# The decay matrix of a head pair: one exponential over 2048 columns in place of eight pieces

## The chip, the cores and the metric

The kernel runs on one core of a Trainium2 chip. The metric is the device time of one execution in microseconds, lower is better. Three executions of the kernel before took 2666.51, 2668.19 and 2668.41 us (median 2668.19).

## What is computed

One step of a hybrid encoder trunk (one layer here) over 384 token columns: one prompt of 256 tokens and eight running streams of 16 tokens. A combined projection gives a pooling branch, a state-space branch (SSD) and gates; both branches are projected, gated, added and projected again, and a squared-ReLU MLP follows. The part that matters here is the SSD scan, in which every head's products of C and B are weighted by a decay:

```
def step(h, inp):
    xc, dtc, Bc, Cc = inp
    cum = jnp.cumsum(dtc * A, axis=1)
    seg = cum[:, :, None] - cum[:, None, :]
    decay = jnp.exp(jnp.where(causal, seg, -jnp.inf))
    cb = jnp.einsum('btgn,bsgn->btsg', Cc, Bc)
    xdt = xc * dtc[..., None]
    y = jnp.einsum('btsgr,bsgrp->btgrp', cb[..., None] * decay, xdt)
    ...
```

There are 64 heads in 8 groups of 8; a head has 64 channels and a state of 128. A gated RMSNorm with SiLU(z) follows. All data are float32.

## The kernel before, in words

**Weights and matmuls.** Every weight block (128x1024 float32) is fetched by SyncE, then split in two parts: `wh` is a copy on ScalarE (ACT, L70) and `wl` the difference on VectorE (DVE, L71). TensorE (PE) multiplies wh by the high and low part of the activations and wl by the high part (L97 to L100 for projections with stationary weights, L149 to L151 for those with moving weights). There are three buffers each for the raw block, wh and wl. `take` keeps up to three split blocks ahead of the one in use, so the split of a block is called two blocks before its use.

**The SSD stage.** A loop over 8 head groups `g` runs, per group, ten projections (`x` for the conv: four blocks of channels, B and C; then four `z` projections) of two weight blocks each. Between the projections stand the small steps of the scan, each for a pair of column tiles (`Pair`, four heads; two pairs a group). The second pair of a group is finished at the head of the next group, the last one after the loop, around `gate_b`. PE's order is written out by hand: each lump of small matmuls and each half projection is put behind the one before (`chain`, `behind`, `lump`). The order on ACT and DVE comes from a planner, which takes the program's order as priority and fills in an instruction when its inputs are ready by the planner's own costs; so it is not the program's order. Each engine runs its list in order.

**The decay matrix E** (`eside`, L751 to L768). For a pair, E is 128x4x512: four heads, 512 columns each. Columns 0:128 are prompt half one with itself, 128:256 half one's influence on half two, 256:384 half two with itself, 384:512 the streams. `eside(S, q)` makes two of the four heads (q is 0 or 1). Its input `cbc` holds the running sum `cum` of the two heads, spread over the partitions by a DMA through DRAM that ACT's queue issues (`cload`). `tok` holds values per token and head; its rows 0 to 2 are cum of the three token blocks, row 9 is `nb`, made in `dt_phase` (L499), row 10 exp(cum) of the streams. Per head, columns 128:256 are Exp with the bias of row 9 (L756), and the other three blocks are Relu(tok - cbc), which keeps the differences from being negative (L758). Then Exp(-E) goes over columns 0:128 of the two heads (L766) and over columns 256:512 of the two (L767), and DVE multiplies the two heads by the masked products `cbm` (L768). E has one buffer, so the first write of a pair's E waits for the matmuls of the pair before (`t_Y`, L677), which read it.

**Where eside is called.** For the first pair of a group: `eside(S, 0)` after the last conv projection, `eside(S, 1)` after the projection z0, and `t_Y` after z3. For the second pair: `eside(.., 0)` after the next group's first conv projection, `eside(.., 1)` after its second, `t_Y` after its fifth. After the last group both are called one behind the other, ahead of `gate_b(0)`.

**Other instructions on the same queues.** ACT runs conv taps (L590), Silu of the conv (L596) and of z (L919), copies (L582 to L584) and the splits; when a function is not in the table set that is loaded, a table load (ACT_TABLE_LOAD) stands before it under the same line. DVE runs evacuations of PSUM (L576, L918), conv taps (L592), the scaling of the state by its decay (L771), its update (L794) and the splits.

**Transpositions through DRAM.** x and B are transposed in 32x32 blocks on DVE (L607), written to DRAM and read back by DMAs that GpSimd (POOL) issues (L612, L618).

Of the kernel before, what the change touches and what calls it, by code (L numbers as in the profile page):

```python
# [9 lines left out]
AF = mybir.ActivationFunctionType  # L10
ALU = mybir.AluOpType
# [3 lines left out]
P = 128  # L15
T = 384
TP = 256
# [16 lines left out]
def build(ctx, tc, io):  # L34
    nc = tc.nc
    v, s, te, gp, sy = nc.vector, nc.scalar, nc.tensor, nc.gpsimd, nc.sync
# [13 lines left out]
    def mmtile(name):  # L50
        return psm.tile([P, 512], F32, tag="mm", name=name)
# [4 lines left out]
    def behind(ins):  # L56
        return nullcontext() if ins is None else tc.issue_after(ins.ins)
# [24 lines left out]
    def woven(a):  # L82
        return a.rearrange("p (a n) -> p n a", a=2)

    def pairs(a):
        return a.rearrange("p (n a) -> p n a", a=2)

    def even_odd(a):
        return a.rearrange("p (n a) -> p a n", a=2)

    def halves(a):
        return a.rearrange("p (a n) -> p a n", a=2)
# [265 lines left out]
    tok = small.tile([P, 11, NH], F32, name="tok")  # L358
    decb = small.tile([P, NH, NB], F32, name="decb")
    with tc.tile_pool(name="phc", bufs=1, reuse_waits="tile") as pc, tc.tile_pool(name="phc2", bufs=2, reuse_waits="tile") as pc2:  # L360
# [3 lines left out]
        for i in range(2):  # L364
            b = pc.tile([P, 640], F32, name=f"pbuf{i}")[:, :519]
# [91 lines left out]
        def dt_phase(pb):  # L457
            ps = mmtile("pj_dt")[:, :T]
            for q in range(2):
                w = wpool.tile([P, 1024], F32, tag="w", name=f"w_dt{q}")  # L460
                hl = wpool.tile([P, 8, 2, NH], F32R, tag="wh", name=f"wh_dt{q}")
                wv = w[:, :512].rearrange("p (k n) -> p k n", k=8)
                sy.dma_start(w[:, :512], io["w_dt"][q])
                s.activation(hl[:, :, 0], wv, AF.Copy)
                v.tensor_tensor(hl[:, :, 1], wv, hl[:, :, 0].bitcast(F32), ALU.subtract)
                for k in range(8):
                    c = hl[:, k].rearrange("p a n -> p (a n)")
                    te.matmul(pairs(ps), c, woven(xg[q * 8 + k][0]), start=q + k == 0, stop=False)
                    te.matmul(pairs(ps), c, woven(xg[q * 8 + k][1]), start=False, stop=q * 8 + k == KD - 1)
            n64 = lambda nm: pb.tile([NH, T], F32, name=nm)  # L470
            dtb = vec[:NH, V_DTB : V_DTB + 1]
            alog = vec[:NH, V_ALOG : V_ALOG + 1]
            raw, ab, e, t1, t2, q = (n64(x) for x in ("raw", "ab", "e", "t1", "t2", "q"))
            nA = pb.tile([NH, 1], F32, name="nA")
            with behind(s.copy(halves(raw), even_odd(ps[NH:]))):
                s.activation(nA, alog, AF.Exp)
            v.tensor_tensor(halves(raw), even_odd(ps[:NH]), halves(raw), ALU.add)
            v.tensor_tensor(raw, raw, rstd[:NH], ALU.mult)
            s.activation(ab, raw, AF.Abs, bias=dtb)
            s.activation(e, ab, AF.Exp, scale=-1.0)  # L480
            v.tensor_scalar(t1, e, 2.0, None, ALU.add)
            v.reciprocal(t2, t1)
            v.tensor_tensor(t1, e, t2, ALU.mult)
            v.tensor_tensor(t2, t1, t1, ALU.mult)
            v.tensor_scalar(q, t2, 1.0 / 19.0, None, ALU.mult)
            for i in range(8, 0, -1):
                v.scalar_tensor_tensor(out=q, in0=q, scalar=1.0 / (2 * i + 1), in1=t2, op0=ALU.add, op1=ALU.mult)
            v.scalar_tensor_tensor(out=q, in0=q, scalar=1.0, in1=t1, op0=ALU.add, op1=ALU.mult)
            v.tensor_scalar(raw, raw, dtb, 0.0, ALU.add, ALU.max)
            dt, cum = n64("dt"), n64("cum")  # L490
            v.scalar_tensor_tensor(out=dt, in0=q, scalar=2.0, in1=raw, op0=ALU.mult, op1=ALU.add)
            dta, we, dtw = n64("dta"), n64("we"), n64("dtw")
            v.tensor_scalar(dta, dt, nA, -1.0, ALU.mult, ALU.mult)
            v.tensor_tensor_scan(cum, cst[:NH, C_SCAN : C_SCAN + T], dta, 0.0, ALU.mult, ALU.add)
            sy.dma_start(cum_scr, cum)
            nb = n64("nb")
            tot = pb.tile([NH, 1], F32, name="tot")
            v.tensor_tensor(tot, cum[:, 127:128], cum[:, 255:256], ALU.add)
            v.tensor_scalar(nb[:, :P], cum[:, :P], cum[:, 127:128], -1.0, ALU.subtract, ALU.mult)  # L499
            v.tensor_scalar(we[:, :P], cum[:, :P], tot, -1.0, ALU.subtract, ALU.mult)  # L500
            v.tensor_scalar(we[:, P:TP], cum[:, P:TP], cum[:, 255:256], -1.0, ALU.subtract, ALU.mult)
            cs = cum[:, TP:].rearrange("h (b t) -> h b t", b=NB)
            last = cs[:, :, TS_ - 1 : TS_]
            v.tensor_tensor(
                we[:, TP:].rearrange("h (b t) -> h b t", b=NB), last.to_broadcast([NH, NB, TS_]), cs, ALU.subtract
            )
            s.activation(we, we, AF.Exp)
            v.tensor_tensor(dtw, dt, we, ALU.mult)
            s.activation(nb[:, TP:], cum[:, TP:], AF.Exp)
            dec = pb.tile([NH, NB], F32, name="dec")  # L510
            s.activation(dec, last.squeeze(2), AF.Exp)
            sy.dma_start(dec_scr, dec)
            sy.dma_start(decb, dec_scr.partition_broadcast(P))
            srcs = [cum[:, i * P : i * P + P] for i in range(3)] + [dt[:, i * P : i * P + P] for i in range(3)]
            srcs += [dtw[:, i * P : i * P + P] for i in range(3)] + [nb[:, :P], nb[:, TP:]]
            return srcs
# [11 lines left out]
        for gi in range(4):  # L528
            for k4 in range(4):
                pool_tile(gi, k4)  # L530
                if gi and k4 == (gi == 1):
                    if gi == 1:
                        sg = gate_a(0)
                    pool_map(gi - 1, last[0])
        srcs = dt_phase(pc)
        pool_map(3)
        for nb in range(4):
# [18 lines left out]
    with tc.tile_pool(name="phd", bufs=2, reuse_waits="tile") as pd, tc.tile_pool(  # L556
# [5 lines left out]
        for i in range(3):  # L562
            b = pd1.tile([P, 24, 19], F32, name=f"cbuf{i}")
# [187 lines left out]
        def eside(S, q):  # L751
            if q == 0:
                S.E = pd.tile([P, 4, 512], F32, tag="E", name=f"E{S.nm}", bufs=1)
            for hh in (q * 2, q * 2 + 1):
                ch = S.cbcs[q][:, hh % 2]
                s.activation(S.E[:, hh, P:TP], ch[:, P:TP], AF.Exp, bias=tok[:, 9, S.h0 + hh : S.h0 + hh + 1])  # L756
                for b, e0 in enumerate((0, TP, T)):
                    s.activation(  # L758
                        S.E[:, hh, e0 : e0 + P],
                        ch[:, b * P : b * P + P],  # L760
                        AF.Relu,
                        bias=tok[:, b, S.h0 + hh : S.h0 + hh + 1],
                        scale=-1.0,
                    )
            Eq = S.E[:, q * 2 : q * 2 + 2]
            s.activation(Eq[:, :, :P], Eq[:, :, :P], AF.Exp, scale=-1.0)  # L766
            s.activation(Eq[:, :, TP:], Eq[:, :, TP:], AF.Exp, scale=-1.0)  # L767
            v.tensor_tensor(Eq, Eq, S.D.cbm.unsqueeze(1).to_broadcast([P, 2, 512]), ALU.mult)  # L768

        def dside(S):  # L770
            v.tensor_tensor(  # L771
# [79 lines left out]
        for g in range(G + 1):  # L851
            if g == G:
                xside(prev.p[1])
                eside(prev.p[1], 0)
                eside(prev.p[1], 1)
                dside(prev.p[1])
                gate_b(0, pd, "hs")
                py = mmtile("pp_last")
                lump(lambda: t_pp(prev.p[1], py))
                lump(lambda: t_yT(prev.p[1]))  # L860
                lump(lambda: t_Y(prev.p[1]))
                state(prev.p[1])
                final(prev.p[1])
                gate_b(1, pd, "hs")
                finish(prev)
                break
# [9 lines left out]
            if g:  # L876
                eside(prev.p[1], 0)
# [14 lines left out]
            S = D.p[0]  # L892
# [383 lines left out]
    with tc.tile_pool(name="phg", bufs=1, reuse_waits="tile") as pg, tc.tile_pool(  # L1276
# [9 lines left out]
        for c8 in range(NC):  # L1286
            hh = []
# [175 lines left out]
```

## Time and profile before

| what | value |
|---|---|
| median of three executions | 2668.19 us |
| the profiled execution, its own time | 2666.41 us |
| its span, first to last instruction | 2664.6 us |
| granted TensorE clock, mean | 0.999 |
| SSD stage and closing part, about | 420 to 1310 us of the span |
| one steady head group | 90 us, of which PE 89.3, DVE 77, ACT 61, POOL 25 |

How to read it: the busy row gives each engine's share of the span; the views of waits say which engine stood idle before which instruction, and until what; PEld are the weight loads of PE, which run beside its matmuls. A row of the timeline is the start, the duration, the engine, the line, the operation, what it writes and reads, and in brackets the idle time before it and what ended that.

### The profile page before, as it was taken

The page shows a single profiled execution, that of the slowest core. Times are in us where ns is not written, and L with a number is a line of the kernel's source. Part 1 is how long each engine was busy: PE and PEld are TensorE (multiplying, and loading weights), DVE is VectorE, ACT ScalarE, POOL GpSimd, SP SyncE. Part 2 cuts the span into 40 slices and gives each one's busy share as a digit, 9 for nine tenths or more (in the row PEclk, how much of TensorE's full clock was granted, in tenths as well). Part 3 has the DMA queues.
Part 4 walks back from the last instruction along what each step waited for, and adds up shares of the span by engine and source line. Part 5 has one row for each costly group of instructions (what it writes and reads, how often), then busy time and mean ns, then how long its engine had stood idle before and what let it go on. Part 6 is the DMA issues. An engine that isn't in the chain of part 4 may idle for free.

```text
span 2664.6 us, 38740 instructions
## 1 busy us (share of the span) xinstructions
PE 2639.9 (99%) x15405; PEld 2454.2 (92%) x15405; DVE 1528.4 (57%) x2148; ACT 1196.3 (45%) x1850; POOL 226.6 (9%) x350
## 2 busy tenths in 40 slices
PE   9999999999999999999999999999999999999998
PEld 9998888999999999978888888999999999999897
DVE  6585335788888988856334446534444444444446
ACT  6443225567676767645322235533233333323233
POOL 0000001223222322210000000000000000000000
PEclk9999999999999999999999999999999999999999
DMA  7444446556666666747544544444444444444443
GB/s 272 150 135 155 147 146 218 182 194 223 216 221 202 218 224 212 240 163 246 178 158 158 175 169 133 148 135 135 136 135 138 137 135 134 135 135 135 136 137 131
DMA packets 129141, 451.37 MB, mean 169 GB/s; under 512 B 17408, under 2 KB 24128, under 8 KB 123968
## 3 DMA queue, kind: packets, MB, share of 16 engines
q1 hardware_dynamic: 103552, 361.57, 41.2%
q0 software_dynamic: 18496, 72.64, 7.6%
q10 hardware_dynamic: 6912, 14.68, 1.7%
q8 instruction: 121, 1.98, 0.3%
q14 instruction: 60, 0.49, 0.1%
HBM read 404.49 MB, written 44.34 MB: 168 GB/s over the span
## 4 chain that ended last, share of the span: by engine, by line
PE 74%; issue 14%; DVE 7%; ACT 3%; DMA 1%; POOL 1%; DVEq 0%; ACTq 0%; POOLq 0%
PE pj_up L98 6%; PE pj_up L100 6%; PE pj_up L99 6%; PE wd L151 6%; PE wd L150 6%; PE wd L149 6%; PE pj_x L98 3%; PE pj_x L99 3%; PE pj_x L100 3%; PE pj_sp L150 3%; PE pj_sp L149 3%; PE pj_sp L151 3%; PE pj_z L100 2%; PE wo L151 2%; PE wo L149 2%
## 5 line engine op out<-in xcount | busy, mean ns | idle before, releaser
L98 PE MATMUL pj_up<-x1h,wh_up 128*128 128x384 f32 (+1 forms) x1024 | 333.7, 326 | 0.0
L99 PE MATMUL pj_up<-x1l,wh_up 128*128 128x384 f32 (+1 forms) x1024 | 333.4, 326 | 0.0
L100 PE MATMUL pj_up<-x1h,wl_up 128*128 128x384 f32 (+1 forms) x1024 | 333.4, 326 | 0.0
L71 DVE TENSOR_TENSOR wl_wd<-w_wd,wh_wd 128x1024 fp32r<-128x1024 f32 x126 | 154.4, 1225 | 240.4 <-ACT wh_wd L70 240.4
L149 PE MATMUL wd<-wh_wd,hh 128*128 128x512 f32 x756 | 286.5, 379 | 0.0
L150 PE MATMUL wd<-wl_wd,hh 128*128 128x512 f32 x756 | 286.5, 379 | 0.0
L151 PE MATMUL wd<-wh_wd,hl 128*128 128x512 f32 x756 | 286.5, 379 | 0.0
L70 ACT ACTIVATE wh_wd<-w_wd 128x1024 fp32r<-128x1024 f32 x126 | 133.1, 1057 | 322.2 <-PE wd L151 261.8
L70 ACT ACTIVATE wh_up<-w_up 128x1024 fp32r<-128x1024 f32 x126 | 133.1, 1057 | 292.2 <-PE pj_up L99 231.8
L71 DVE TENSOR_TENSOR wl_up<-w_up,wh_up 128x1024 fp32r<-128x1024 f32 x126 | 154.4, 1225 | 178.3 <-ACT wh_up L70 178.2
L98 PE MATMUL pj_x<-xgh,wh_x 128*128 128x384 f32 x768 | 252.0, 328 | 0.6 <-ACT wh_x L70 0.6
L100 PE MATMUL pj_x<-xgh,wl_x 128*128 128x384 f32 x768 | 250.6, 326 | 1.1 <-DVE wl_x L71 1.1
L99 PE MATMUL pj_x<-xgl,wh_x 128*128 128x384 f32 x768 | 250.4, 326 | 0.0
L99 PEld LDWEIGHTS pj_up<-x1l,wh_up 128*128 128x128 f32 x1024 | 193.6, 189 | 0.2
L98 PEld LDWEIGHTS pj_up<-x1h,wh_up 128*128 128x128 f32 x1024 | 193.6, 189 | 0.2
L100 PEld LDWEIGHTS pj_up<-x1h,wl_up 128*128 128x128 f32 x1024 | 193.6, 189 | 0.0
L100 PE MATMUL pj_z<-xgh,wl_z 128*128 128x384 f32 x512 | 168.6, 329 | 6.3 <-DVE wl_z L71 5.6
L98 PE MATMUL pj_z<-xgh,wh_z 128*128 128x384 f32 x512 | 167.4, 327 | 0.0
L99 PE MATMUL pj_z<-xgl,wh_z 128*128 128x384 f32 x512 | 166.9, 326 | 0.0
L71 DVE TENSOR_TENSOR wl_sp<-w_sp,wh_sp 128x1024 fp32r<-128x1024 f32 x64 | 78.4, 1225 | 154.0 <-ACT wh_sp L70 154.0
L151 PEld LDWEIGHTS wd<-wh_wd,hl 128*128 128x128 f32 x756 | 142.9, 189 | 20.3
L149 PEld LDWEIGHTS wd<-wh_wd,hh 128*128 128x128 f32 x756 | 142.9, 189 | 20.1
(335 smaller groups left out, 5997.0 us busy)
## 6 DMA issues: line engine op xcount, KB each, us to landing
w_up<-w_up SPq DMA_DIRECT2D x128, 512.0 KB, 3.4
w_wd<-w_down SPq DMA_DIRECT2D x128, 512.0 KB, 3.4
w_x<-w_in SPq DMA_DIRECT2D x96, 512.0 KB, 4.4
w_z<-w_in SPq DMA_DIRECT2D x64, 512.0 KB, 4.5
w_sp<-w_ssd SPq DMA_DIRECT2D x64, 512.0 KB, 3.4
w_ga<-w_ga SPq DMA_DIRECT2D x32, 512.0 KB, 3.4
w_pp<-w_pp SPq DMA_DIRECT2D x32, 512.0 KB, 3.4
hs<-ssm POOLq DMA_DIRECT2D x16, 1024.0 KB, 7.4
```

The lines of the kernel that those rows point to most:

```text
L70: cut[0] = s.activation(h, w, AF.Copy)
L71: cut[1] = v.tensor_tensor(l, w, h.bitcast(F32), ALU.subtract)
L98: te.matmul(out, wh, xh, start=first, stop=False, **how)
L99: te.matmul(out, wh, xl, start=False, stop=False, **how)
L100: return te.matmul(out, wl, xh, start=False, stop=last, **how)
L149: te.matmul(out, mh, vh, start=k == 0, stop=False)
L150: te.matmul(out, mh, vl, start=False, stop=False)
L151: last[0] = te.matmul(out, ml, vh, start=False, stop=k == nk - 1)
```

## The change

`eside` now makes all of E's pre-exponential blocks by Relu, columns 128:256 too: for that, `nb` keeps its sign (cum of the token less cum at position 127) and serves as the bias of a Relu like the others. The exponentials per half are gone. When the second half (q = 1) has been filled, one Exp goes over all 2048 columns of the pair, and the two multiplies by cbm follow it.

```
@@ dt_phase
-            v.tensor_scalar(nb[:, :P], cum[:, :P], cum[:, 127:128], -1.0, ALU.subtract, ALU.mult)
+            v.tensor_scalar(nb[:, :P], cum[:, :P], cum[:, 127:128], None, ALU.subtract)
@@ eside
             for hh in (q * 2, q * 2 + 1):
                 ch = S.cbcs[q][:, hh % 2]
-                s.activation(S.E[:, hh, P:TP], ch[:, P:TP], AF.Exp, bias=tok[:, 9, S.h0 + hh : S.h0 + hh + 1])
-                for b, e0 in enumerate((0, TP, T)):
+                for row, t0, e0 in ((0, 0, 0), (9, P, P), (1, P, TP), (2, TP, T)):
                     s.activation(
                         S.E[:, hh, e0 : e0 + P],
-                        ch[:, b * P : b * P + P],
+                        ch[:, t0 : t0 + P],
                         AF.Relu,
-                        bias=tok[:, b, S.h0 + hh : S.h0 + hh + 1],
+                        bias=tok[:, row, S.h0 + hh : S.h0 + hh + 1],
                         scale=-1.0,
                     )
-            Eq = S.E[:, q * 2 : q * 2 + 2]
-            s.activation(Eq[:, :, :P], Eq[:, :, :P], AF.Exp, scale=-1.0)
-            s.activation(Eq[:, :, TP:], Eq[:, :, TP:], AF.Exp, scale=-1.0)
-            v.tensor_tensor(Eq, Eq, S.D.cbm.unsqueeze(1).to_broadcast([P, 2, 512]), ALU.mult)
+            if q:
+                s.activation(S.E, S.E, AF.Exp, scale=-1.0)
+                for h2 in (slice(0, 2), slice(2, 4)):
+                    Eq = S.E[:, h2]
+                    v.tensor_tensor(Eq, Eq, S.D.cbm.unsqueeze(1).to_broadcast([P, 2, 512]), ALU.mult)
```

## The prediction

> **What bounds the kernel now.** First the page's busy row, to see which engine has no room; then TensorE's weight loads and what they waited for, in three stretches: the seven steady head groups (510 to 1140 us), the first group (420 to 510) and the closing part (1140 to 1310).
>
> ```profile
> span 2664.6 us, 38740 instructions
> PE 2639.9 (99%) x15405; PEld 2454.2 (92%) x15405; DVE 1528.4 (57%) x2148; ACT 1196.3 (45%) x1850; POOL 226.6 (9%) x350
> ```
>
> PE is the bound, and the change takes nothing from PE. So time can be won only where PE waits, and lost only where a new wait is made. ACT and DVE have room on average; what counts is their queues in front of a weight split (wh on ACT, then wl on DVE).
>
> ```profile
> PEld pj_z L100 <- DVE wl_z L71: 9.5, 14, 1.0
> ```
> ```profile
> PEld cb L647 <- ACT xs L596: 1.8, 1, 1.8
> PEld pj_x L100 <- DVE wl_x L71: 1.7, 2, 1.2
> PEld pj_z L100 <- DVE wl_z L71: 1.5, 2, 0.8
> PEld pj_x L98 <- ACT wh_x L70: 0.9, 1, 0.9
> ```
> ```profile
> PEld pj_gb L149 <- DVE hs L794: 4.6, 2, 2.5
> PEld pj_gb L150 <- DVE wl_gb L71: 1.3, 1, 1.3
> ```
>
> The columns are total us, times, longest. The steady groups lose 9.5 us in 14 waits, two in each group, both in the z projections. The first group loses 1.8 + 1.7 + 1.5 + 0.9 = 5.9. In the closing part 4.6 belong to the state update, which the change does not touch, and 1.3 to a split. All that the change could win is therefore 9.5 + 5.9 + 1.3 = 16.7 us.
>
> The weight loads one by one show the larger wait of each group, here its first and last instance of seven:
>
> ```profile
> 579.76 0.19 PEld L100 LDWEIGHTS pj_z<-xgh,wl_z 128*128 128x128 f32 x1 [0.96 <-DVE wl_z L71]
> ...
> 1119.89 0.19 PEld L100 LDWEIGHTS pj_z<-xgh,wl_z 128*128 128x128 f32 x1 [0.96 <-DVE wl_z L71]
> ```
>
> The 0.96 recurs every 90 us, 7 x 0.96 = 6.7 us; the smaller ones make the other 2.8, 0.4 each. Now ACT ahead of the larger wait, in the group between the two, where it ends with the split of 668.46 (below):
>
> ```profile
> 660.43 0.41 ACT L766 ACTIVATE E<-E 128x256 f32<-128x256 f32 x1
> 660.73 1.05 ACT L70 ACTIVATE wh_z<-w_z 128x1024 fp32r<-128x1024 f32 x1
> ...
> 661.80 1.28 ACT L596 ACT_TABLE_LOAD   x1
> 663.09 0.62 ACT L596 ACTIVATE xs<-cacc,vec 128x384 f32<-128x384 f32 x1
> 663.73 1.28 ACT L767 ACT_TABLE_LOAD   x1
> ...
> 665.02 0.63 ACT L767 ACTIVATE E<-E 128x512 f32<-128x512 f32 x1
> 665.67 1.28 ACT L919 ACT_TABLE_LOAD   x1
> 666.96 0.52 ACT L919 ACTIVATE zs<-zs 128x384 f32<-128x384 f32 x1
> 667.39 1.99 ACT L70 ACTIVATE wh_z<-w_z 128x1024 fp32r<-128x1024 f32 x2
> ```
>
> ACT is unbroken here: three table loads (Silu, Exp, Silu) for three short functions, and the next weight split stands behind them until 667.39. And DVE:
>
> ```profile
> 655.80 1.21 DVE L71 TENSOR_TENSOR wl_z<-w_z,wh_z 128x1024 fp32r<-128x1024 f32 x1
> ...
> 657.47 1.20 DVE L768 TENSOR_TENSOR E<-E,cbm 128x1024 f32<-128x1024 f32 x1
> ```
> ```profile
> 668.46 2.36 DVE L71 TENSOR_TENSOR wl_z<-w_z,wh_z 128x1024 fp32r<-128x1024 f32 x2 [1.56 <-ACT wh_z L70]
> ```
>
> The split of 668.46 had waited 1.56 us for ACT: the 0.96 is ACT's doing. The smaller wait ends with the split of 655.80, at 657.01. No idle time stands in front of that split, so DVE was busy with other work until then and ACT was not waited for; the multiply on E comes after it.
>
> **The change part by part.**
>
> ```profile
> L758 ACT ACTIVATE E<-cbc,tok 128x128 f32<-128x128 f32 x192 | 63.2, 389 | 0.0
> L756 ACT ACTIVATE E<-cbc,tok 128x128 f32<-128x128 f32 x64 | 25.2, 394 | 2.1 <-PE Y L677 1.8
> L767 ACT ACTIVATE E<-E 128x512 f32<-128x512 f32 x32 | 19.8, 619 | 0.1
> L766 ACT ACTIVATE E<-E 128x256 f32<-128x256 f32 x32 | 12.9, 404 | 0.0
> L768 DVE TENSOR_TENSOR E<-E,cbm 128x1024 f32<-128x1024 f32 x32 | 38.8, 1212 | 6.5 <-ACT E L767 6.5
> L756 ACT ACT_TABLE_LOAD x24 | 30.8, 1283 | 0.3
> L596 ACT ACT_TABLE_LOAD x24 | 30.8, 1283 | 0.6 <-ACT ysq L822 0.2
> L767 ACT ACT_TABLE_LOAD x7 | 9.0, 1283 | 0.1
> L919 ACT ACT_TABLE_LOAD x7 | 9.0, 1283 | 0.1
> ```
> ```profile
> L323 ACT ACTIVATE xt<-xt x3: 1895/1908/1912, 22.0 to 32.9; 128x2048 f32<-128x2048 f32 x3
> ```
>
> *Arithmetic on ACT.* There are 16 pairs. The 64 exponentials of L756 become 64 Relus of the same shape (394 against 389 ns): nothing. The wait of a pair's first write to E for the matmuls that read the last one (1.8 us in L756's row) passes to a Relu. Per pair 2 x 404 + 2 x 619 = 2046 ns of exponentials go and one over 2048 columns comes. No row shows Exp of that width; the square over 2048 columns takes 1908 ns, and the other bound is the four present ones, 2046. I take 1.9: 0.1 us less a pair, nothing on the path.
>
> *Table loads.* L758, the Relus, has no group of loads of its own, so only Exp and Silu switch. Now 24 + 7 = 31 loads come before E's exponentials and 31 before Silu, about two of each a pair. With one exponential a pair it is at most 16 and about 16: some 30 fewer, 30 x 1.283 = 38 us of ACT. On the path this is worth only the waits behind it.
>
> *The wait of 0.96.* Leave the order as it is and put the wide exponential where L767 stands (665.02). Ahead of 661.80, L766 and L767 of the first half and L766 of the second go: 0.40 + 0.61 + 0.41 less overlaps of about 0.1 each, 1.1 us. The Silu load of 661.80 goes too, as no Exp came before: -1.28. The exponential grows from 0.63 to 1.9: +1.27. So the split comes 1.1 us sooner than 667.39, and 1.1 > 0.96. This is the tightest placement. But the Relus need no table, so they fit into idle time earlier, and the exponential may then run before the Silu of 663.09, as the second half's L766 already ran before 666.96 although the program has it behind; then the margin is some 3 us more. The multiply leaves 657.47 and both run after the exponential; the program has them behind the splits that the first z projection calls, where the first one was ahead. I take all of it: -6.7; ends -6.7 and 0.
>
> The Trainium skill ("ScalarE: Activation LUTs", section "What ACT_TABLE_LOAD costs") charges every switch a drain of about 1380 ns on top of the 1283. Here the load of 661.80 starts 0.02 us after the weight split ends and Silu starts 0.01 us after the load, so no such drain is seen and I keep 1.28; by the page the margin would be an estimated 2.5 us instead of 1.1, the sum the same.
>
> *The smaller wait* stays: 0; ends -2.8 and, if both multiplies are put in front of that split, 7 x 2 x 1.21 = +16.9.
>
> *The second pair of a group* runs its E at the head of the next group, where Exp is loaded once already. There the pieces become a block of 1.28 + 1.9 = 3.2 us. The split nearest to it:
>
> ```profile
> 696.09 1.22 DVE L768 TENSOR_TENSOR E<-E,cbm 128x1024 f32<-128x1024 f32 x1
> ```
> ```profile
> 699.89 1.22 DVE L71 TENSOR_TENSOR wl_x<-w_x,wh_x 128x1024 fp32r<-128x1024 f32 x1
> ```
> ```profile
> 702.20 0.33 PE L100 MATMUL pj_x<-xgh,wl_x 128*128 128x384 f32 x1
> ```
>
> It ends at 701.11, 1.1 us before PE reads it, and the multiply of 696.09 moves from before it to after it, which gives 1.2 more. I take 0; ends 0 and 7 x 1 = +7, if a block stands in front of it and eats 3.2 of 2.3.
>
> *First group.* Its 5.9 come from the same queue. Of ACT's 433 to 457 us, unbroken, 5 x 1.283 = 6.4 us are table loads; one Silu load stays and the wide exponential brings two, so two go, 2.6 us, with three short exponentials for a wide one in exchange. I take 2.5 of the 5.9; ends -5.4 and +1.5 (the new block, 3.2, less 1.7 of pieces).
>
> *Closing part.* The split behind the last multiply waits 1.3 us. If the planner puts the two multiplies, now later, in front of it, 1.3 becomes 1.3 + 1.2 + 1.1; if it uses DVE's hole before the exponential is done, the 1.3 go. Ends +2.3 and -1.3; I take 0, between them.
>
> *DMAs.* None is added. The load of the next pair's cbc is issued on ACT's queue behind the Relus and perhaps behind the block, 3.2 us later at most; its Relus start only in the next group. The change to nb is the same DVE instruction with one operation less: 0.
>
> **Sum.** -6.7 - 2.5 = -9.2 us on the profiled execution's 2666.41 (span 2664.6 and 1.8 around it): 2657.2. The median of the three runs is 2668.19, 1.8 above that execution, so the forecast for a median is 2659.0.
>
> **The rivals.** *The wait moves with the block (no real change).* Exp, its load and the load back still stand in front of the split and the shorter queue is used up. For it: they are 1.28 + 1.9 + 1.28 = 4.5 us in one piece. Against: the 1.1 us above. It keeps the 6.7, leaving -2.5: about 2666.
>
> *The two multiplies go in front of a split (slower).* Place: DVE, before the split of 655.80, which PE already waits for. It decides when ACT has finished the wide exponential before about 655, which the removed table loads make possible. Price: 2.42 us x 7 = +16.9, less the 6.7 and the 2.5: +7.7, about 2676. Against: the split stands earlier in the program than these multiplies.
>
> *All small waits go.* If the freed ACT also lets the split of 655.80 run before the DVE work ahead of it: -2.8 - 1.3 more, 2655.
>
> **How the numbers follow.** Forecast 0.5, all small waits 0.1, no real change 0.22, slower 0.18. A measurement tells some 0.2% from no change, 5.3 us: 2662.9 to 2673.5. Forecast and the better case fall below: with a little taken off for a first group that gives nothing and a closing part that costs, faster 0.57; same 0.25; slower 0.18. The range goes from 2653 to 2673: the better ends of the forecast (first group -5.4) below, no change and a partial new wait above; the full slower case stays out. The forecast's own range is 2654 to 2664.
>
> **What would show it.** Exp table loads on E: 16, in all about 32 where 62 stood. In the waits of the weight loads between 510 and 1140 us, pj_z for wl_z: 7 times some 0.4, the 0.96 gone. E's Exp at about 1.9 us. In the first group fewer than 3.5 us of waits. I am wrong if pj_x or pj_z shows a new wait behind a multiply or behind the 2048-column instruction, repeated seven times.

## The result and the profile after

| | before | after |
|---|---|---|
| median, runs on the same chip | 2667.13 us (18 runs, 2665.08 to 2669.43) | 2671.47 us (18 runs, 2669.18 to 2677.13) |
| ratio, 95% interval | | 1.0019 [1.0012, 1.0027] |
| profiled execution, own time | 2666.41 us | 2669.18 us |

The change makes the kernel 4.3 us slower, 0.19%, where 2659.0 was forecast: a small loss, but of the other sign. The page after, its first lines:

```profile
span 2667.2 us, 38669 instructions
...
PE 2637.9 (99%) x15405; PEld 2452.3 (92%) x15405; DVE 1526.7 (57%) x2148; ACT 1157.6 (43%) x1771; POOL 225.8 (8%) x350
```

ACT has 38.7 us less to do (1196.3 before), and nothing came of it. The groups of E after (ACT and DVE, 400 to 1200 us) say that the work itself changed as foreseen:

```profile
L757 ACT ACTIVATE E<-cbc,tok 128x128 f32<-128x128 f32 x256 | 80.1, 388 | 20.0 <-PE Y L677 20.0
L765 ACT ACTIVATE E<-E 128x2048 f32<-128x2048 f32 x16 | 30.8, 1923 | 0.2
L596 ACT ACT_TABLE_LOAD x16 | 20.5, 1283 | 0.3
L765 ACT ACT_TABLE_LOAD x16 | 20.5, 1283 | 0.3
```
```profile
L768 DVE TENSOR_TENSOR E<-E,cbm 128x1024 f32<-128x1024 f32 x32 | 38.8, 1216 | 2.3 <-ACT E L765 2.3
```

32 table loads stand where 62 stood. To see where the time went, take three matmuls that stand at the same place of PE's order in both kernels: the end of the first group (py), the norm near the end of the last steady group (bc_g) and the last state product (pp_last). Before, and then after:

```profile
508.20 1.08 PE L656 MATMUL py<-hs,Cm 128*32 128x256 f32 x16
...
1127.47 0.33 PE L196 MATMUL bc_g<-nh_g,onesr 128*128 128x384 f32 x1
...
1174.94 0.83 PE L691 MATMUL pp_last<-xhl,Bhl 128*128 128x256 f32 x6
```
```profile
509.27 1.08 PE L656 MATMUL py<-hs,Cm 128*32 128x256 f32 x16
...
1131.16 0.33 PE L196 MATMUL bc_g<-nh_g,onesr 128*128 128x384 f32 x1
...
1177.49 0.83 PE L691 MATMUL pp_last<-xhl,Bhl 128*128 128x256 f32 x6
```

After is 1.07 us late at the first, 3.69 at the second, 2.55 at the third, and still 2.6 at the end of the span. So the stretches give +1.1 (up to the first group's end), +2.6 (steady groups) and -1.1 (closing part), where -2.5, -6.7 and 0 were forecast. The medians differ by some 1.7 us more than these two traces. In both traces the clock that TensorE was granted is full up to 2650 us (no slice of 2 us below 0.99); of after's 18 runs, the seven with a mean clock of 0.999, the traced one among them, average 2670.7 us, the other eleven 2673.1. Only stretches of traces are compared below.

PE's weight loads and their waits after, in the same three stretches as before (us in total, times, longest):

```profile
PEld pj_x L100 <- DVE wl_x L71: 4.1, 3, 2.7
PEld pj_x L98 <- ACT wh_x L70: 2.1, 2, 1.4
PEld cb L647 <- ACT xs L596: 1.1, 1, 1.1
...
PEld pj_z L100 <- DVE wl_z L71: 12.5, 13, 1.5
...
PEld pj_gb L149 <- DVE hs L794: 4.6, 2, 2.5
```

The steady groups wait 12.5 us where it was 9.5, and the longest wait is 1.5 where it was 0.96. It is not the same wait. Here is the group that the prediction showed, on PEld, ACT and DVE:

```profile
657.89 0.19 PEld L100 LDWEIGHTS pj_z<-xgh,wl_z 128*128 128x128 f32 x1 [0.43 <-DVE wl_z L71]
...
663.25 0.19 PEld L100 LDWEIGHTS pj_z<-xgh,wl_z 128*128 128x128 f32 x1 [1.49 <-DVE wl_z L71]
```
```profile
655.39 1.28 ACT L765 ACT_TABLE_LOAD   x1
656.69 1.92 ACT L765 ACTIVATE E<-E 128x2048 f32<-128x2048 f32 x1
...
659.30 1.99 ACT L70 ACTIVATE wh_z<-w_z 128x1024 fp32r<-128x1024 f32 x2
...
662.38 1.28 ACT L596 ACT_TABLE_LOAD   x1
...
664.28 1.04 ACT L70 ACTIVATE wh_z<-w_z 128x1024 fp32r<-128x1024 f32 x1
```
```profile
656.62 1.21 DVE L71 TENSOR_TENSOR wl_z<-w_z,wh_z 128x1024 fp32r<-128x1024 f32 x1
...
658.64 1.23 DVE L768 TENSOR_TENSOR E<-E,cbm 128x1024 f32<-128x1024 f32 x1 [0.27 <-ACT E L765]
659.78 0.61 DVE L592 SCALAR_TENSOR_TENSOR cacc<-cbuf,vec,cacc 128x384 f32<-128x384 f32 x1
660.31 1.22 DVE L768 TENSOR_TENSOR E<-E,cbm 128x1024 f32<-128x1024 f32 x1
661.45 0.61 DVE L592 SCALAR_TENSOR_TENSOR cacc<-cbuf,vec,cacc 128x384 f32<-128x384 f32 x1
661.98 1.22 DVE L71 TENSOR_TENSOR wl_z<-w_z,wh_z 128x1024 fp32r<-128x1024 f32 x1
```

The split that PE waited 0.96 us for (z2's first half) is in time now: its wh starts on ACT at 664.28 and not at 667.39. But the block of load and exponential stands in front of the split *before* it (z1's first half). Its wh starts at 659.30 where it was 656.45 (0.8 of that is the lateness of the whole group, as 656.62 against 655.80 shows), and while DVE could not have that split, both multiplies came in front of it. The wh is done at about 660.3 (the row holds two halves in 1.99 us); DVE takes the split at 661.98, a multiply and a tap later, and PE waits 1.49.

### The profile page after: what moved, and what is told of

Its sections match the earlier page's. It is cut to its first block, busy times and chain, and to the rows that moved or that the text cites. A ratio compares the mean times of both kernels' runs of the same rounds, so it can differ in the third digit from the quotient of the medians.

```text
span 2667.2 us, 38669 instructions
## 1 busy us (share of the span) xinstructions
PE 2637.9 (99%) x15405; PEld 2452.3 (92%) x15405; DVE 1526.7 (57%) x2148; ACT 1157.6 (43%) x1771; POOL 225.8 (8%) x350
## 4 chain that ended last, share of the span: by engine, by line
PE 79%; issue 14%; DVE 3%; ACT 2%; DMA 1%; POOL 1%; SPq 0%; DVEq 0%; POOLq 0%; ACTq 0%
PE pj_up L98 6%; PE pj_up L99 6%; PE pj_up L100 6%; PE wd L151 6%; PE wd L150 6%; PE wd L149 6%; PE pj_x L98 4%; PE pj_x L99 4%; PE pj_x L100 4%; PE pj_sp L151 3%; PE pj_sp L149 3%; PE pj_sp L150 3%; PE pj_z L100 2%; PE pj_z L99 2%; PE pj_z L98 2%
```

## The experiments

Two theories for the steady groups. D: the two multiplies, in one piece on DVE in front of z1's split, make the new wait. A: the block on ACT, 3.2 us in front of the same split's wh, makes it, and the multiplies only fill DVE's idle time. All edits but f1 and g2 are to the changed kernel; ratios are to runs of the kernel before on the same chip, 16 to 33 of them. The next three columns are stretches between the matmuls named above, in us against the trace before (start to py, py to bc_g, bc_g to the end). The last column is explained below the table.

| kernel | median us | ratio, 95% interval | first group | steady groups | closing | slow clock: first, closing |
|---|---|---|---|---|---|---|
| after | 2671.47 | 1.0019 [1.0012, 1.0027] | +1.1 | +2.6 | -1.1 | 0, 0 |
| e1: multiplies behind the split | 2665.14 | 0.9990 [0.9981, 0.9998] | +5.0 | -6.2 | +0.9 | 1.7, 1.7 |
| e2: exponential and multiplies behind it | 2668.89 | 1.0007 [0.9998, 1.0016] | +6.8 | -6.0 | +2.3 | 3.4, 1.5 |
| e3: an exponential of 1024 at each call | 2665.26 | 0.9992 [0.9983, 1.0000] | +4.1 | -9.4 | +2.1 | 3.4, 1.7 |
| e4: two of 1024 at the second call | 2663.32 | 0.9986 [0.9977, 0.9995] | +0.1 | -6.8 | +2.7 | 1.7, 0 |
| f1: before, multiplies behind the split | 2666.99 | 0.9999 [0.9990, 1.0008] | -0.7 | +0.1 | 0.0 | 0, 0 |
| f2: after, first pair's Relus held back | 2672.92 | 1.0021 [1.0012, 1.0030] | +2.0 | +3.4 | +0.5 | 1.7, 1.7 |
| f3: e4 with the edit of f2 | 2663.80 | 0.9988 [0.9979, 0.9997] | +1.3 | -6.9 | +2.4 | 1.7, 0 |
| f5: e3 with the edit of f2 | 2661.94 | 0.9982 [0.9974, 0.9991] | +0.4 | -9.5 | +6.1 | 0, 4.9 |
| g1: f5, last norm later | 2658.68 | 0.9969 [0.9957, 0.9980] | +1.9 | * | * | 3.4, 0 |
| g2: before, both multiplies at the second call | 2666.49 | 0.9997 [0.9988, 1.0006] | -0.6 | 0.0 | +0.5 | 0, 1.7 |

\* g1 moves the bc_g that is the mark; its span is 8.3 us shorter than before's (2656.3 against 2664.6).

The first group and the closing part hold more than waits. In most of these traces the granted clock falls there to 0.50 for some 3.4 us at a time, after a wait of PE: in e1, behind a wait of 4.1 us, it is 0.70, 0.50 and 0.94 in the three slices of 2 us from 456 on, which costs 1.7 us. The last column gives what each trace loses in this way; it is an upper bound, as a slow stretch can overlap with a wait. Before, after and f1 have none there, and no trace has one in the steady groups: only that column can be read as waits alone. The wait by itself does not decide it: behind the same two waits of 1.4 and 1.0 us in the first group, e4 has a slow stretch and after has none; behind the same 2.5 us in the closing part, g2 has one and before has none. What decides it stays open, so that a difference of the size of the last column is no proof for or against an edit.

### e1, e2: what stands behind the split

`later()` puts an instruction behind the last weight split that the program has called. e1 wraps the multiplies in it, e2 the exponential as well.

```
@@ eside (e1)
-                    v.tensor_tensor(Eq, Eq, S.D.cbm...to_broadcast([P, 2, 512]), ALU.mult)
+                    with later():
+                        v.tensor_tensor(Eq, Eq, S.D.cbm...to_broadcast([P, 2, 512]), ALU.mult)
@@ eside (e2)
             if q:
-                s.activation(S.E, S.E, AF.Exp, scale=-1.0)
-                for h2 in (slice(0, 2), slice(2, 4)):
...
+                with later():
+                    s.activation(S.E, S.E, AF.Exp, scale=-1.0)
+                    for h2 in (slice(0, 2), slice(2, 4)):
...
```

> Only the two multiplies by cbm are put behind the last weight split called so far (DVE order alone; the wide exponential stays where it is). Theory (DVE): the steady groups lose 1.5 us each at the first half of projection z1 because both multiplies, 1.2 us each, run on DVE before its wl split. Then this wait goes: weight loads of pj_z waiting for wl_z between 510 and 1140 us fall from 12.5 us to about 3 (the 0.4 of z0 stays), and the time falls by some 9 us from 2671.5 to about 2662, 0.2% under before. Rival (ACT): the load and the wide exponential, 3.2 us in one piece, make the wh split late and that alone holds PE. Then the wait stays above 1 us a group, the sum at 9 or more, and the time at 2669 to 2672.

> The wide exponential too is put behind the last weight split called so far, on ACT, and the two multiplies on DVE. By either theory the wait at z1 goes (pj_z sum about 3 us or less). First group: if its 7.3 us of waits (before: 5.9) come from the block of load, exponential and load between 443 and 448 us, they fall to 4 or less, and the time goes to about 2658 to 2660; if they come from elsewhere, they stay at 6 to 7.5 and the time is that of the run with the multiplies alone moved, about 2662.

DVE of e1 in the same group, and its waits from 510 to 1130 us:

```profile
662.75 1.27 DVE L592 SCALAR_TENSOR_TENSOR cacc<-cbuf,vec,cacc 128x384 f32<-128x384 f32 x2 [1.07 <-ACT cacc L590]
663.94 1.22 DVE L71 TENSOR_TENSOR wl_z<-w_z,wh_z 128x1024 fp32r<-128x1024 f32 x1
...
665.61 1.22 DVE L71 TENSOR_TENSOR wl_z<-w_z,wh_z 128x1024 fp32r<-128x1024 f32 x1
666.74 1.22 DVE L769 TENSOR_TENSOR E<-E,cbm 128x1024 f32<-128x1024 f32 x1
...
668.37 1.19 DVE L769 TENSOR_TENSOR E<-E,cbm 128x1024 f32<-128x1024 f32 x1
```
```profile
PEld pj_z L100 <- DVE wl_z L71: 2.8, 7, 0.4
```

The block on ACT is where it was (load and exponential at 658.71, 3.3 us behind after's 655.39, as the whole group is by then), and the waits of 1.5 are gone with the multiplies. So D holds and A falls: the split can bear the block on ACT, but not block and multiplies. The steady groups are worth -6.2 in e1, close to the -6.7 of the forecast; the median is 2665.1 and not the expected 2662, because the first group gives 3.9 us of it back against after's. Moving the exponential as well (e2) gains nothing there, and its first group missed the expectation: some 10 us of waits.

### e3, e4: smaller pieces

```
@@ eside (e3)
-            if q:
-                s.activation(S.E, S.E, AF.Exp, scale=-1.0)
-                for h2 in (slice(0, 2), slice(2, 4)):
-                    Eq = S.E[:, h2]
-                    v.tensor_tensor(Eq, Eq, S.D.cbm...to_broadcast([P, 2, 512]), ALU.mult)
+            Eq = S.E[:, q * 2 : q * 2 + 2]
+            s.activation(Eq, Eq, AF.Exp, scale=-1.0)
+            v.tensor_tensor(Eq, Eq, S.D.cbm...to_broadcast([P, 2, 512]), ALU.mult)
@@ eside (e4)
             if q:
-                s.activation(S.E, S.E, AF.Exp, scale=-1.0)
                 for h2 in (slice(0, 2), slice(2, 4)):
                     Eq = S.E[:, h2]
+                    s.activation(Eq, Eq, AF.Exp, scale=-1.0)
```

> Relu for all four blocks as in the change, but one exponential of 1024 columns and one multiply per half, each in its own call as before. Theory (DVE): not two multiplies stand together in front of a split any more, so the 1.5 us at z1 go; pj_z sum 3 us or less, time 2657 to 2663. Rival (ACT): two pieces of 1.1 us and a load stand in the queue, 3.4 us in all, and the waits stay above 9 us in sum, time 2668 or more. Rival (Relu): if the Relu in place of Exp for columns 128:256 is itself what costs, nothing changes from 2671.

> As the change, but the wide exponential is cut into two of 1024 columns, each followed by its multiply, all still when the second half is filled. One multiply then stands in front of the wl split of z1, not two. Theory (DVE): the 1.5 us become about 0.3 (1.2 less), pj_z sum 12.5 to about 5, time about 2664 to 2666. Rival (ACT): ACT's work in front of the wh split is the same or 0.2 us longer, so the waits stay at 12 and the time at 2671.

e4 has the Relus, the second call and all the multiplies of the change; only the exponential is cut in two. DVE of e4 in the same group, and its waits from 510 to 1130 us:

```profile
656.61 1.21 DVE L768 TENSOR_TENSOR E<-E,cbm 128x1024 f32<-128x1024 f32 x1
657.74 1.21 DVE L71 TENSOR_TENSOR wl_z<-w_z,wh_z 128x1024 fp32r<-128x1024 f32 x1
...
659.41 1.21 DVE L768 TENSOR_TENSOR E<-E,cbm 128x1024 f32<-128x1024 f32 x1
```
```profile
PEld pj_z L100 <- DVE wl_z L71: 2.9, 7, 0.4
```

With one multiply in front of the split and the other behind it, PE does not wait for it; the waits fell further than expected (2.9, where 5 was). e4 alone does not part multiplies from ACT: its table load and first exponential now run from 649.53 on, ahead of the split, and z1's wh starts 4.1 us sooner, at 655.22 (1.7 of that is the lead of the whole group). That the wait goes when only the multiplies move is shown by e1. What costs is thus the width: one exponential over all four heads keeps both multiplies back and then releases them close together in front of the split. The table loads are nearly as few as in the change (17 + 17 in place of 16 + 16). e3 spreads the multiplies further and has no pj_z wait left at all in the steady groups; it gains 9.4 us there and gives 4 and 2 back in the first group and the closing part, slow stretches included, so that its median is 2665.3 where 2657 to 2663 was expected.

### f1, g2: the same moves in the kernel before

```
@@ eside of the kernel before (f1)
-            v.tensor_tensor(Eq, Eq, S.D.cbm...to_broadcast([P, 2, 512]), ALU.mult)
+            with later():
+                v.tensor_tensor(Eq, Eq, S.D.cbm...to_broadcast([P, 2, 512]), ALU.mult)
@@ eside of the kernel before (g2)
-            v.tensor_tensor(Eq, Eq, S.D.cbm...to_broadcast([P, 2, 512]), ALU.mult)
+            if q:
+                for h2 in (slice(0, 2), slice(2, 4)):
+                    Eq = S.E[:, h2]
+                    v.tensor_tensor(Eq, Eq, S.D.cbm...to_broadcast([P, 2, 512]), ALU.mult)
```

> The kernel before, with its own four short exponentials and all its table loads, only that its multiply by cbm may not run ahead of the last weight split that the program has called. It separates the two things that differ between the kernel before and e1: the exponential and the place of the multiplies. If the gain of e1 in the steady groups (pj_z waits 2.8 us in place of 9.5) comes from the table loads that are gone, then here the wait of 0.96 stays, because it ends with a weight split that waits for ACT: 510 to 1140 us shows pj_z for wl_z at 6.7 to 9.5 us, about 2667. If the place of the multiplies is all that counts, pj_z falls to about 3 us here too, about 2661 to 2663.

> The kernel before, its short exponentials and table loads kept, only with both multiplies at the second call of a pair, as in the change. If moving the multiplies there is harmful by itself, the split of z1's first half gets them in front of it as in the changed kernel: pj_z for wl_z at 12.5 us or more, 2670 or slower. If it takes the finished wide exponential to bring both in front, at most one multiply gets there and pj_z stays between 9.5 and 12.5 us: 2667 to 2670.

Neither moves the kernel before. The waits of f1 from 510 to 1130 us:

```profile
PEld pj_z L100 <- DVE wl_z L71: 9.6, 14, 1.0
```

So the 0.96 is ACT's doing, as the prediction read it, and e1's gain needs what the change does on ACT. g2 has 9.5 us there (expected 9.5 to 12.5) and DVE's order of before: one multiply at 656.85, the split at 658.51, the other multiply only at 665.07, when ACT is done with its half. Calling both multiplies late does no harm; that needs an exponential that frees both before the split can run.

### f2, f3, f5: the first group

After, the first group waits 7.3 us (4.1 + 2.1 + 1.1) where it was 5.9. Its longest, 2.7, ends with a split that stands on DVE behind a step waiting for a DMA:

```profile
449.99 0.56 DVE L741 TENSOR_TENSOR xdt<-xT,tok 128x384 f32<-128x384 f32 x1 [4.43 <-DMA xT<-t_scr]
...
451.56 1.18 DVE L71 TENSOR_TENSOR wl_x<-w_x,wh_x 128x1024 fp32r<-128x1024 f32 x1
```

Its wh had been put behind the block on ACT (448.67), and so xdt came in front of its wl. The edit keeps the first pair's Relus, and with them the block, behind the splits:

```
@@ eside (f2)
-                for row, t0, e0 in ((0, 0, 0), (9, P, P), (1, P, TP), (2, TP, T)):
...
+                with later() if S.h0 == 0 else nullcontext():
+                    for row, t0, e0 in ((0, 0, 0), (9, P, P), (1, P, TP), (2, TP, T)):
...
```

> The changed kernel, only that the 16 Relus of the very first pair (head group 0) may not run ahead of the last weight split called; the order of the steady groups stays that of the changed kernel. Theory: in the first group the Relus and the block of load, exponential and load, pulled forward between the splits of x, make the wait there (7.3 us between 420 and 510). Then that falls to 4 us or less, pj_z stays near 12.5 us in the steady groups, and the time is 2667 to 2669. Rival: the late transposed x (a DVE instruction that waits for its DMA in front of a split) makes it: pj_x for wl_x stays at about 4 us, and the time at 2671.

> e4 (two exponentials of 1024 columns at the end, each followed by its multiply) with the edit of f2. If the two losses are separate, they add up: steady groups as in e4 (pj_z about 2.9 us), first group 4 us or less as in f2: 2660 to 2663. If the first group of e4 was at its floor with 4.3 us, nothing is left: 2663.

> e3 (Relus throughout, one exponential of 1024 columns and one multiply at each call) with the edit of f2. Steady groups as in e3 (no pj_z wait), first group 4 us or less where e3 had 8: 2659 to 2662, the fastest of all. Rival: PE then meets the closing part sooner and waits there for something that does not move (2.4 us in e3 at 1137 us, more here): 2664.

f2 missed. Its waits from 410 to 510 us:

```profile
PEld cb L647 <- ACT xs L596: 2.6, 1, 2.6
PEld pj_x L100 <- DVE wl_x L71: 1.8, 2, 1.0
PEld pj_x L98 <- PE py L656: 1.3, 1, 1.3
PEld pj_x L98 <- ACT wh_x L70: 0.8, 1, 0.8
```

The 2.7 is gone (split ahead of xdt: pj_x for wl_x 1.8), but the wait for cb grew. The 1.3 behind py belongs to the slow clock: py's 16 matmuls take 1.96 us where after's take 1.09, and the granted clock is 0.63 and 0.52 in the two slices of 2 us from 464 on. Without it 5.2 us of waits are left, where after has 7.3 and 4 or less was expected, and the stretch is no shorter than after's: the slow clock took back about what the edit saved. f3 is no faster than e4. f5's span (2661.6 us) equals e3's (2661.5): its first group, without a slow stretch, is 3.7 us shorter, its closing part 4.0 longer. So over the whole kernel the edit is worth nothing that these traces show, although f5's median is lower.

### g1: where the closing part gives it back

e2, e3, e4, f3 and f5 lose 2 to 6 us behind bc_g. In f5 the first gate matmul waits. Its weight load and its matmul name different releasers:

```profile
1135.30 0.29 PEld L149 LDWEIGHTS pj_gb<-wh_gb,xgh 128*128 128x128 f32 x1 [4.29 <-ACT E L758]
```
```profile
1135.33 0.77 PE L149 MATMUL pj_gb<-wh_gb,xgh 128*128 128x512 f32 x1 [4.13 <-DVE xs L808]
```
```profile
1125.39 0.35 DVE L182 TENSOR_SCALAR ny_g<-ssum 128x384 int32<-128x384 int32 x1
...
1132.47 2.19 DVE L829 SCALAR_TENSOR_TENSOR zs<-zs,vec,ny_g 128x384 f32<-128x384 f32 x4
1134.58 1.13 DVE L808 SCALAR_TENSOR_TENSOR xs<-xs,vec,Y 128x384 f32<-128x384 f32 x2
```

The Relus of L758 ended at 1134.6, 0.7 us before the wait did. L808 is DVE's last read of Y in PSUM, and it stands behind the norm of the group before (1125.39 to 1134.66). Before, DVE's reads ended at 1140.1 and PE was there at 1140.2, without a wait.

The wait is only part of the 6.1 us that f5 loses here. Its weight loads wait 8.3 us in the closing part where before's wait 5.9, which makes 2.4. The rest is the clock, 0.50 and 0.52 in the two slices of 5 us from 1135 on, where before has 1.00; the gate matmuls start 0.43 us apart until 1144.8, and 0.21 or 0.22 from then on:

```profile
1142.65 0.63 PE L150 MATMUL pj_gb<-wl_gb,xgh 128*128 128x512 f32 x1
1143.08 0.63 PE L151 MATMUL pj_gb<-wh_gb,xgl 128*128 128x512 f32 x1
...
1147.37 0.38 PE L149 MATMUL pj_gb<-wh_gb,xgh 128*128 128x512 f32 x1
1147.58 0.38 PE L150 MATMUL pj_gb<-wl_gb,xgh 128*128 128x512 f32 x1
```

g1 calls that norm (`finish`) after the last state update:

```
@@ the group loop (g1)
             zproj(2)
-            if g:
+            if 0 < g < G - 1:
                 finish(prev)
...
             final(S)
+            if g == G - 1:
+                finish(prev)
             prev = D
```

> f5 with one step of the closing part moved: the norm of head group 6 (ten short DVE instructions and four scalings) is called after the first state update of group 7 and not before its last z projection. In f5 the first gate matmul waits 4.3 us at 1131 us. Theory: it waits for the PSUM tile of Y, which DVE reads (xs, L808) only behind that norm. Then the wait goes or shrinks to 1 us and the span falls by 2 to 4 us: 2658 to 2660. Rival: it waits for something that this does not move (the first gate weights, whose DMA landed at 1123 us, or the exponential that the trace names): the 4.3 us stay, 2662.

g1's waits from 1130 us on:

```profile
PEld pj_gb L149 <- DVE hs L793: 5.0, 2, 3.0
```

The 4.3 is gone, and with it the slow stretch. The first gate matmul starts at 1132.72, just behind DVE's reads of Y (to 1131.73) and while the Relus still run (1130.66 to 1134.47), so it was not the Relus that held it. The span falls by 5.3 us against f5, more than the 2 to 4 expected, as the clock came back too, although g1's first group has slow stretches that f5's has not (+1.9 against +0.4). g1 is the fastest kernel of the study, 0.9969 [0.9957, 0.9980] of before and 12.8 us under the change by the medians. What its last edit would do to the kernel before was not tried.

## Why the prediction was wrong, point by point

**What bounds the kernel: right.** PE's own time hardly changed (2637.9 against 2639.9), and in these two traces gain and loss lie in the waits of its weight loads: +1.4, +3.0 and -1.3 us in the three stretches. What the prediction has no term for is the slow clock that a wait can bring; these two traces have none, most of the experiments have.

**Arithmetic and table loads: right.** Relus at 388 ns, the wide exponential at 1923 (1.9 taken), 32 loads (about 32). The load of 655.39 starts as Bm's copy ends (655.38), and the exponential 0.02 us after it: no drain of 1.38 us on top, so on this the trace stays against the page "ScalarE: Activation LUTs" of the Trainium skill (section "What ACT_TABLE_LOAD costs").

**The wait of 0.96: its reading right, the step on the multiplies wrong.** That ACT's queue makes it is confirmed by f1, and it is gone after. The step that failed is this one: "both run after the exponential; the program has them behind the splits that the first z projection calls, where the first one was ahead. I take all of it: -6.7". The program's order was taken for DVE's order. But the same block that went earlier on ACT put z1's wh later, and with that split not ready and E ready, both multiplies were filled in before it. In place of -6.7 the steady groups gave +2.6; with only the multiplies put where the prediction had them (e1) they give -6.2. The prediction moved the exponential earlier "then the margin is some 3 us more" for z2's split and did not ask which split it would then stand in front of.

**The rival that came.** It was "the two multiplies go in front of a split (slower)", with its condition, an exponential done early because the table loads are gone. Place and price were off: not the split of 655.80 but the one behind it, which had some time in hand, so 1.5 a group and not 2.4; 2676 was its price, 2671.5 came. Its chance of 0.18 was too low for a reason that the prediction had in hand: it had just shown a second-half exponential running ahead of its place in the program, and gave as the argument against that the split stands earlier in the program.

**The smaller wait: right** at 0. 0.43 in place of 0.37, at the same split. It goes only in e3, f5 and g1.

**The second pair: right** at 0; no pj_x wait appears in the steady groups.

**The first group: wrong sign.** -2.5 was taken because two table loads go there; the stretch came +1.1. The two loads did go (five before and three after between 433 and 457 us), but the longest wait, 2.7 us, is set by the order around the late transposed x and not by ACT's total. f2 took 2.1 us of waits out and lost about as much to a slow stretch of the clock. Which order would win there stays open; e4's and f5's come closest to before's (+0.1 and +0.4).

**The closing part: within its ends.** 0 was taken between +2.3 and -1.3; it came -1.1, the 1.3 us wait for the gate split being gone.

**Range and chances.** 2671.5 lies inside 2653 to 2673, near its upper end, and the loss of 0.19% just short of what was called measurable; but the likeliest case had the wrong sign.

## What to carry to other kernels

Merging short instructions into a wide one takes time off the engine's total, but it also releases everything behind it at one moment; look at what becomes ready then and which due instruction it gets in front of, on the other engine too. Where a planner fills instructions in as they become ready, the program's order is no evidence for an instruction's place: if its place matters, tie it (e1) or keep the pieces small enough to go to either side (e3, e4). A gain upstream is kept only if the next fixed meeting point moves as well: f5 won 9.5 us and lost 6.1 of it, in waits for a PSUM read queued behind a norm and in slow matmuls after them, until g1 moved the norm. And look at the granted clock before a stretch is put down to waits alone.

## What the hardware showed unexpectedly

Exp on 128 partitions takes 404 ns for 256 columns (before), about 1.05 us for 1024 (e4) and 1923 for 2048: from the two ends (1923 - 404) / 1792 = 0.85 ns a column and some 187 ns fixed. The four pieces that the wide exponential replaces took 2046 ns, 123 more than it does, or 2 us over 16 pairs: nearly all of the 38.7 us that ACT saves are table loads.

A wait of PE can cost more than its length: in nine of the twelve traces the granted clock falls to 0.50 behind some waits, and one such stretch of 3.4 us costs 1.7 (e1 at 456 us).

The releaser that a view names need not be the same for a weight load and for its matmul: in f5 they name ACT's Relu and DVE's read of Y for the same wait, and g1 shows that it was not the Relu.
